# Four pass units of a decoder layer: float32 products replaced by split products, with the rests of their weights made on GpSimd

## The chip, the cores and the metric

The kernel runs on one core of a Trainium2 chip. Five engines each work through a queue of their own, in order: TensorE (PE, with its weight loads shown apart as PEld), VectorE (DVE), ScalarE (ACT), GpSimd (POOL) and SyncE (SP, which here only issues transfers). The metric is the device time of one execution in microseconds (us); lower is better. The median of three runs of the kernel before is 1585.19 us (1583.76 to 1586.9).

## The reference, cut to what matters

One decoder layer on 256 tokens of width 2048, all in float32: a conditioning vector gives six shift, scale and gate vectors, a normed and modulated input goes through one wide projection, and its parts feed a recurrent branch and an attention branch; then come an output projection and an MLP.

```python
mod = jnp.dot(c_act, w_ada[l]) + b_ada[l]
shift1, scale1, gate1, shift2, scale2, gate2 = jnp.split(mod, 6, axis=-1)
h = _modulate(_rms_norm(x, norm1_g[l]), shift1, scale1)
proj = jnp.einsum("bsd,de->bse", h, w_in[l])
lru_x, lru_gate, q, k, v, g_a, g_b = jnp.split(proj, split_idx, axis=-1)
...
```

The change is in the first part of `proj`: some products of `h` with columns of `w_in`.

## The kernel before

**Split products.** A float32 matrix product is put together from three products. Weights `w` and activations `h` are each split in a rounded part and a rest (`wh`, `wl` and `h[:, 0]`, `h[:, 1]`, of type float32r). `gemm` (lines 179 to 188) issues per tile of 128 rows `wh`·`h[:,0]` (L185), `wh`·`h[:,1]` (L186) and `wl`·`h[:,0]` (L187). The rounded half of a weight chunk of 128x1024 is made on ScalarE (`w_round`, L160), the rest `wl = raw - wh` on VectorE (`w_rest`, L165). `gemm_native` (L214) is the other way: it multiplies the raw weights with the unsplit activations `xs` in plain float32, with no preparation at all. In the trace each of its products shows as two records.

**The passes.** The conditioning matrix `w_ada` comes in 96 pieces of 1 MB, and each gives one column of `mod` on VectorE (`ada_unit`, L299). Tile j of `h` needs columns of two pieces: then `a` on VectorE (L314), the modulation and the rounding on ScalarE (L316, L318), the rest on VectorE (L322). While these tiles come into being one by one, TensorE already multiplies with those that exist. This is done in three passes over parts of the depth: tiles 0 and 1, tiles 2 to 5, tiles 6 to 9, for 56, 56 and 40 output tiles. A *pass unit* is one load of 1 MB of weights (2048 columns in `raw`, two chunks) for 16 products: pass one has units 0 to 6, pass two units 7 to 20 (four output tiles by four depth tiles each), pass three units 21 to 30. The table `NATIVE` names four units of pass two, with first output tile 0, 16, 32 and 48: units 7, 11, 15 and 19. They go through `gemm_native`. All others are split: `w_split` of the next unit is called one unit ahead. The sums of a unit leave PSUM (four buffers, `pg`) by VectorE in passes two and three (L399, L401).

**What sets the order.** Each engine's order is fixed when the program is built, by a scheduler that starts from the order of the code. Buffers come in rings: four for `raw` (weights and pieces of `w_ada` share them, names `rw` and `ra`), four each for `wh` and `wl`, so that two units are in the making or in use at a time. SyncE issues the loads; a load waits until the buffer's last user is done: for a split unit that is the rest's maker, for a native unit its last product.

**Behind the passes** comes `rel_lines` (lines 352 to 361): three small transfers issued from ScalarE's queue (L357), among them `onehot`, and a small product (L359) that needs them. Then the rest of the projection's depth follows from `w_r`, first for k and v.

Of the kernel before, what the change touches and what calls it, by code (L numbers as in the profile page):

```python
# [10 lines left out]
F32 = mybir.dt.float32  # L11
F32R = mybir.dt.float32r
AF = mybir.ActivationFunctionType
ALU = mybir.AluOpType
# [24 lines left out]
ZN_FROM = 9  # L39

PASSES = [(0, 2, 56), (2, 6, 56), (6, 10, 40)]
NATIVE = {(2, u) for u in range(0, 56, 16)}
NATIVE_REST = set()

ADA_ORDER = ([j + KT * s for j in range(KT) for s in (0, 1)] + [KT * s + j for s in (2, 4, 3, 5) for j in range(KT)])
# [13 lines left out]
def hybrid_layer(ctx: ExitStack, tc: tile.TileContext, x, xt, wada, w_p, w_r, w_f, vec, lruw, relb,  # L59
                 onehot, maskc, ident, out):  # L60
    nc = tc.nc
    te, ve, se = nc.tensor, nc.vector, nc.scalar
# [12 lines left out]
    def nm(s):  # L75
        cnt[0] += 1
        return f"{s}{cnt[0]}"

    def pair(dt=F32):
        return kp.tile([P, 2, T], dt, tag="k2", name=nm("k"))  # L80

    def tmp(shape=(P, 2, T), dt=F32):
        return tp.tile(list(shape), dt, tag="t2", name=nm("t"))
# [5 lines left out]
    pin = tc.keep_in_program_order  # L89
# [63 lines left out]
    def w_dma(src, n, pin=lambda i: i):  # L153
        raw = wp.tile([P, 2048], F32, tag="raw", name=nm("rw"), bufs=RAW_BUFS)
        pin(nc.sync.dma_start(out=raw[:, :n], in_=src))
        return raw, n

    def w_round(raw, o, c, pin=lambda i: i):
        wh = wp.tile([P, WCH], F32R, tag="wh", name=nm("wh"), bufs=WH_BUFS)
        pin(se.activation(wh[:, :c], raw[:, o:o + c], AF.Copy))  # L160
        return wh

    def w_rest(raw, o, c, wh, pin=lambda i: i):
        wl = wp.tile([P, WCH], F32R, tag="wl", name=nm("wl"), bufs=WH_BUFS)
        pin(ve.tensor_tensor(out=wl[:, :c], in0=raw[:, o:o + c], in1=wh[:, :c].bitcast(F32), op=ALU.subtract))  # L165
        return wh, wl

    def w_split(raw, n, pin=lambda i: i, o0=0):
        parts = []
        for o in range(o0, o0 + n, WCH):  # L170
            c = min(WCH, o0 + n - o)
            parts.append(w_rest(raw, o, c, w_round(raw, o, c, pin), pin))
        return parts

    def w_load(src, n):
        return w_split(*w_dma(src, n))

    def gemm(parts, o, acts):
        ps = pg.tile([P, T], F32, tag="pg", name=nm("pg"))
        n = len(acts)  # L180
        for k, hl in enumerate(acts):
            e = (o + k) * P
            wh, wl = parts[e // WCH]
            w = slice(e % WCH, e % WCH + P)
            te.matmul(ps, lhsT=wh[:, w], rhs=hl[:, 0], start=k == 0, stop=False)  # L185
            te.matmul(ps, lhsT=wh[:, w], rhs=hl[:, 1], start=False, stop=False)  # L186
            te.matmul(ps, lhsT=wl[:, w], rhs=hl[:, 0], start=False, stop=k == n - 1)  # L187
        return ps
# [20 lines left out]
    def gemm_native(raw, o, k0, k1):  # L209

        ps = pg.tile([P, T], F32, tag="pg", name=nm("pg"))
        for k in range(k0, k1):
            e = (o + k - k0) * P
            te.matmul(ps, lhsT=raw[:, e:e + P], rhs=xs[k // 2][:, k % 2], start=k == k0, stop=k == k1 - 1)  # L214
        return ps
# [50 lines left out]
    def turn_in(q, pin=lambda i: i):  # L266

        for j in (2 * q, 2 * q + 1):
            px = bank([P, 512])
            for i in range(2):  # L270
                for b in range(2):
                    e = (2 * (j % 2) + i) * P
                    te.transpose(px[:, i * T + b * P:i * T + (b + 1) * P], xtok[b, q][:, e:e + P], idt)
            xs.append(pair())
            pin(se.activation(xs[j].rearrange("p a b -> p (a b)"), px, AF.Copy))
# [27 lines left out]
    h = [None] * KT  # L303
    a1 = cp.tile([P, KT], F32, name="a1")

    def ada_norm1():
        n = ada_unit()
        if n % 2 == 1:
            norm1_tile(n // 2)
            norm1_rest(n // 2)  # L310
# [16 lines left out]
    raws = [w_dma(w_p[0], 2048, pin)]  # L327
# [7 lines left out]
    whs = w_round(raws[0][0], 0, WCH, pin)  # L335
    norm1_tile(0, pin)
    split_w = {0: [w_rest(raws[0][0], 0, WCH, whs, pin)]}
    norm1_rest(0, pin)
    ada_unit(pin)
    raws.append(w_dma(w_p[1], 2048, pin))  # L340
    split_w[0] += w_split(raws[0][0], WCH, pin, WCH)
    ada_unit(pin)
    norm1_tile(1, pin)
# [47 lines left out]
    def add_part(ps, f):  # L391
        sc_q = F_Q <= f < F_LX
        if f not in res:
            if f % 2 == 0:
                cur[0] = pair()
            res[f] = cur[0][:, f % 2]
            se.activation(res[f], ps, AF.Copy, scale=0.125 if sc_q else 1.0)
        elif sc_q:
            ve.scalar_tensor_tensor(out=res[f], in0=ps, scalar=0.125, in1=res[f], op0=ALU.mult, op1=ALU.add)  # L399
        else:  # L400
            ve.tensor_tensor(out=res[f], in0=ps, in1=res[f], op=ALU.add)  # L401


    p_units = [(k0, k1, u, min(KT // (k1 - k0), n - u))
               for k0, k1, n in PASSES for u in range(0, n, KT // (k1 - k0))]

    def pass_dma(i):
        k0, k1, u, nf = p_units[i]
        n = nf * (k1 - k0) * P
        raws.append(w_dma(w_p[i, :, 0:n], n))  # L410

    ada_due = 0.0
    for i, (k0, k1, u, nf) in enumerate(p_units):
        while len(raws) <= min(i + 1, len(p_units) - 1):
            pass_dma(len(raws))
        for j in (i, i + 1):
            if j < len(p_units) and j not in split_w and (p_units[j][0], p_units[j][2]) not in NATIVE:
                split_w[j] = w_split(*raws[j])
        while h[k1 - 1] is None:
            ada_norm1()  # L420
        for f in range(nf):
            kw = k1 - k0
            if (k0, u) in NATIVE:
                add_part(gemm_native(raws[i][0], f * kw, k0, k1), u + f)
            else:
                add_part(gemm(split_w[i], f * kw, h[k0:k1]), u + f)
        raws[i] = split_w[i] = None
        if i == 0:
            turn_in(2)
            turn_in(3)  # L430
        ada_due += ADA_FIRST
        while ada_due > 0 and ada_next[0] < 2 * KT:
            ada_norm1()
            ada_due -= 1
# [438 lines left out]
    for n in range(8):  # L873
        q, b = divmod(n, 2)
        pt = turned[n] if n < 2 else turn(n)
        o = tmp([P, 512])
# [97 lines left out]
```

## Time and profile before

| what | value |
|---|---|
| median of three runs | 1585.19 us |
| the profiled execution: its time, its span | 1588.35 us, 1586.0 us |
| granted TensorE clock, mean | 0.992 |
| HBM traffic over the span | 244 GB/s |
| the native units' first products at | 71.4, 97.05, 120.9 and 144.8 us |

Times in the views are microseconds from the span's start. In a timeline a row gives the start, the length, the engine, the line, the operation, what is written and read, how many were merged, and in brackets how long the engine had stood idle before it and what ended that. In a table of groups, the busy time and the mean of one in ns follow the count, then the idle time before. In a table of windows each engine has its busy time and, in brackets, its instructions; then come the granted clock, the share of the transfer engines and GB/s. A chain lists, in order of time, what the end was waiting for.

### The profile page before, as it was taken

Reading aid. Unit: us, or ns where it says so; the run is one execution under the profiler, and the core shown is the slowest. Engines: PE = TensorE matmul, PEld = TensorE weight load, DVE = VectorE, ACT = ScalarE, POOL = GpSimd, SP = SyncE. Lnnn points to the kernel's source line nnn. Section 1 sums busy time; section 2 is a strip of 40 time slices with the busy share of each in tenths; the row PEclk is TensorE's granted clock in tenths of the full one; section 3 lists DMA queues with packets and bytes.
Section 4 is the critical chain, followed back from the end, with each engine's and each line's share of the span. In section 5 each row is a group of like instructions: output and inputs, shape, how many; then the busy total and the mean of one; then the engine's idle time right before and its main releaser. Section 6 shows DMA issues by size and latency. Waiting matters only on the chain.

```text
span 1586.0 us, 24927 instructions
## 1 busy us (share of the span) xinstructions
PE 1545.5 (97%) x9812; PEld 1385.9 (87%) x9812; DVE 1217.2 (77%) x1941; ACT 886.2 (56%) x1510; POOL 0.2 (0%) x4
## 2 busy tenths in 40 slices
PE   5999999999999999999999999999999999999997
PEld 4999988899988888888889988888888888888886
DVE  6898988899999878789898877965565556655664
ACT  6733437686896564444456763356434663356553
POOL 0000000000000000000000000000000000000000
PEclk7999999999999999999999999999999999999999
DMA  8898976457867768777886666965555555555551
GB/s 343 332 350 333 341 257 224 173 181 244 302 244 282 281 239 313 277 292 285 329 301 239 235 246 244 348 233 186 186 186 188 188 189 187 189 191 191 190 187 54
DMA packets 61413, 387.89 MB, mean 245 GB/s; under 512 B 6800, under 2 KB 11248, under 8 KB 18928
## 3 DMA queue, kind: packets, MB, share of 16 engines
q1 hardware_dynamic: 56016, 380.83, 65.7%
q10 hardware_dynamic: 5280, 5.47, 1.1%
q8 instruction: 77, 1.26, 0.3%
q14 instruction: 40, 0.33, 0.1%
HBM read 384.13 MB, written 2.15 MB: 244 GB/s over the span
## 4 chain that ended last, share of the span: by engine, by line
PE 89%; DVE 5%; DMA 2%; ACT 2%; issue 1%; ACTq 0%; DVEq 0%
PE pg L199 45%; PE pg L198 21%; PE pg L187 5%; PE pg L185 5%; PE pg L186 5%; DVE ra L299 1%; PE pg L201 1%; DVE wl L165 1%; PE pg L214 1%; PE pg L762 1%; PE pg L763 1%; PE pg L764 1%; PE pa L575 1%; PE pa L568 1%; DMA ra<-in_wada_dram 1%
## 5 line engine op out<-in xcount | busy, mean ns | idle before, releaser
L199 PE MATMUL pg<-k,wh 128*128 128x512 f32 x3120 | 1078.9, 395 | 1.1 <-DVE k L149 1.1
L165 DVE TENSOR_TENSOR wl<-rw,wh 128x1024 fp32r<-128x1024 f32 (+2 forms) x534 | 625.9, 1178 | 270.9 <-ACT wh L160 261.3
L198 PE MATMUL pg<-k,wl 128*128 128x256 f32 x2925 | 819.2, 280 | 0.0
L160 ACT ACTIVATE wh<-rw 128x1024 fp32r<-128x1024 f32 (+2 forms) x534 | 542.3, 1021 | 491.3 <-PE pg L199 332.4
L199 PEld LDWEIGHTS pg<-k,wh 128*128 128x128 f32 x3120 | 572.7, 188 | 120.4 <-issue 1.4
L198 PEld LDWEIGHTS pg<-k,wl 128*128 128x128 f32 x2925 | 551.0, 188 | 9.7 <-ACT k L148 0.5
L185 PE MATMUL pg<-k,wh 128*128 128x256 f32 x832 | 238.3, 287 | 11.1 <-ACT k L318 9.7
L187 PE MATMUL pg<-k,wl 128*128 128x256 f32 x832 | 236.4, 284 | 2.1 <-DVE wl L165 2.1
L186 PE MATMUL pg<-k,wh 128*128 128x256 f32 x832 | 236.4, 284 | 0.0
L299 DVE CUSTOM_DVE_ANT_0 ra<-ra,scr,vc 128x2048 f32<-128x2048 f32 x96 | 224.8, 2344 | 4.3 <-DMA ra<-in_wada_dram 4.3
L185 PEld LDWEIGHTS pg<-k,wh 128*128 128x128 f32 x832 | 158.1, 190 | 14.1 <-ACT k L318 10.2
L187 PEld LDWEIGHTS pg<-k,wl 128*128 128x128 f32 x832 | 159.0, 191 | 3.8 <-DVE wl L165 2.7
L186 PEld LDWEIGHTS pg<-k,wh 128*128 128x128 f32 x832 | 158.4, 190 | 1.0 <-issue 0.7
L790 DVE SCALAR_TENSOR_TENSOR k<-pg,mod,k 128x256 f32<-128x256 f32 x128 | 61.9, 483 | 34.2 <-PE pg L199 32.0
L779 ACT ACTIVATE t<-t 128x256 f32<-128x256 f32 x55 | 23.0, 418 | 70.6 <-DVE t L206 70.5
L206 DVE TENSOR_TENSOR t<-pg,t 128x256 f32<-128x256 f32 x131 | 54.6, 417 | 0.3 <-ACT t L205 0.3
L201 PE MATMUL pg<-k,wl 128*128 128x256 f32 x195 | 54.5, 280 | 0.0
L205 ACT ACTIVATE t<-pg 128x256 f32<-128x256 f32 x131 | 47.7, 364 | 0.3 <-PE pg L199 0.3
L201 PEld LDWEIGHTS pg<-k,wl 128*128 128x128 f32 x195 | 36.6, 188 | 8.0
L763 PE MATMUL pg<-z,wh 128*128 128x256 f32 x144 | 40.9, 285 | 0.0
L762 PE MATMUL pg<-z,wh 128*128 128x258 f32 x144 | 40.9, 284 | 0.0
L764 PE MATMUL pg<-z,wl 128*128 128x258 f32 x144 | 40.7, 283 | 0.0
(163 smaller groups left out, 952.8 us busy)
## 6 DMA issues: line engine op xcount, KB each, us to landing
rw<-in_w_f_dram SPq DMA_DIRECT2D x204, 1024.0 KB, 4.9
ra<-in_wada_dram SPq DMA_DIRECT2D x96, 1024.0 KB, 6.3
rw<-in_w_p_dram SPq DMA_DIRECT2D x31, 1024.0 KB, 6.9
rw<-in_w_r_dram SPq DMA_DIRECT2D x20, 768.0 KB, 4.7
rw<-in_w_r_dram SPq DMA_DIRECT2D x16, 640.0 KB, 3.9
bt<-ud ACTq DMA_DIRECT2D x8, 512.0 KB, 3.9
lw<-in_lruw_dram SPq DMA_DIRECT2D x4, 512.0 KB, 5.3
k<-in_x_dram SPq DMA_DIRECT2D x8, 256.0 KB, 5.7
```

Of the source, the lines that this page charges most:

```text
L160: pin(se.activation(wh[:, :c], raw[:, o:o + c], AF.Copy))
L165: pin(ve.tensor_tensor(out=wl[:, :c], in0=raw[:, o:o + c], in1=wh[:, :c].bitcast(F32), op=ALU.subtract))
L185: te.matmul(ps, lhsT=wh[:, w], rhs=hl[:, 0], start=k == 0, stop=False)
L186: te.matmul(ps, lhsT=wh[:, w], rhs=hl[:, 1], start=False, stop=False)
L187: te.matmul(ps, lhsT=wl[:, w], rhs=hl[:, 0], start=False, stop=k == n - 1)
L198: te.matmul(ps[:, 0], lhsT=wl[:, w], rhs=hl[:, 0], start=False, stop=False)
L199: te.matmul(ps, lhsT=wh[:, w], rhs=hl, start=k == 0, stop=k == n - 1)
L201: te.matmul(ps[:, 0], lhsT=wl[:, w], rhs=hl[:, 0], start=False, stop=False)
L299: pin(ve.tensor_tensor_reduce(out=raw, in0=raw, in1=scr, scale=1.0, scalar=vc[:, V_BADA + c:V_BADA + c + 1], op0=ALU.mult, op1=ALU.add, ac ...
L762: te.matmul(ps, lhsT=wh[:, e], rhs=z[k][:, 0:258], start=k == 0, stop=False)
L763: te.matmul(ps[:, 0:256], lhsT=wh[:, e], rhs=z[k][:, 258:514], start=False, stop=False)
L790: ve.scalar_tensor_tensor(out=x1[f], in0=ps[:, i], scalar=mod[:, 5 * KT + f:5 * KT + f + 1], in1=x1[f], op0=ALU.mult, op1=ALU.add)
```

## The change

`NATIVE` becomes `POOL_REST`, and the four units are split like the others. Their rests are subtracted on GpSimd. No other unit's instructions change in kind or number. GpSimd gets eight subtractions of 128x1024, ScalarE eight roundings more, TensorE 192 split products in place of 64 plain ones. VectorE and SyncE have as many instructions as before.

```diff
-NATIVE = {(2, u) for u in range(0, 56, 16)}
+
+POOL_REST = {(2, u) for u in range(0, 56, 16)}
...
-    def w_rest(raw, o, c, wh, pin=lambda i: i):
+    def w_rest(raw, o, c, wh, pin=lambda i: i, eng=nc.vector):
         wl = wp.tile([P, WCH], F32R, tag="wl", name=nm("wl"), bufs=WH_BUFS)
-        pin(ve.tensor_tensor(out=wl[:, :c], in0=raw[:, o:o + c], in1=wh[:, :c].bitcast(F32), op=ALU.subtract))
+        pin(eng.tensor_tensor(out=wl[:, :c], in0=raw[:, o:o + c], in1=wh[:, :c].bitcast(F32), op=ALU.subtract))
         return wh, wl
-    def w_split(raw, n, pin=lambda i: i, o0=0):
+    def w_split(raw, n, pin=lambda i: i, o0=0, eng=nc.vector):
...
-            parts.append(w_rest(raw, o, c, w_round(raw, o, c, pin), pin))
+            parts.append(w_rest(raw, o, c, w_round(raw, o, c, pin), pin, eng))
...
-            if j < len(p_units) and j not in split_w and (p_units[j][0], p_units[j][2]) not in NATIVE:
-                split_w[j] = w_split(*raws[j])
+            if j < len(p_units) and j not in split_w:
+                split_w[j] = w_split(*raws[j], eng=nc.gpsimd if (p_units[j][0], p_units[j][2]) in POOL_REST else ve)
...
-            if (k0, u) in NATIVE:
-                add_part(gemm_native(raws[i][0], f * kw, k0, k1), u + f)
-            else:
-                add_part(gemm(split_w[i], f * kw, h[k0:k1]), u + f)
+            add_part(gemm(split_w[i], f * kw, h[k0:k1]), u + f)
```

The new file has one line more above these places, so that L165 becomes L166, L299 becomes L300 and so on; the texts below keep the numbers of the kernel before.

The scheduler also moves instructions of the other engines, from unit 7 to the middle of the projection's remaining depth. Two places matter below. The first is VectorE at unit 7. `wl_829` and `wl_833` are the rests of unit 8, the `ra` are pieces of `w_ada` (each with the reading of its sum, `ISA mod`), `a_153` and `k_843` belong to depth tile 5. Before:

```order
L165 TENSOR_TENSOR wl_829<-rw_825,wh_827 128x1024
L165 TENSOR_TENSOR wl_833<-rw_825,wh_831 128x1024
L299 ISA ra_835,mod<-ra_835,scr,vc 128x2048
L299 ISA ra_838,mod<-ra_838,scr,vc 128x2048
L314 SCALAR_TENSOR_TENSOR a_153<-mod,vc 128x1
L299 ISA ra_870,mod<-ra_870,scr,vc 128x2048
L322 TENSOR_TENSOR k_843<-k_215,k_843 128x256
```

The same place in the changed kernel, where the rests of unit 8 are called `wl_837` and `wl_841` and tile 5's is `k_851`:

```order
L166 TENSOR_TENSOR wl_837<-rw_833,wh_835 128x1024
L166 TENSOR_TENSOR wl_841<-rw_833,wh_839 128x1024
L300 ISA ra_843,mod<-ra_843,scr,vc 128x2048
L300 ISA ra_846,mod<-ra_846,scr,vc 128x2048
L300 ISA ra_910,mod<-ra_910,scr,vc 128x2048
L315 SCALAR_TENSOR_TENSOR a_153<-mod,vc 128x1
L323 TENSOR_TENSOR k_851<-k_215,k_851 128x256
```

A third piece of `w_ada` now stands ahead of `a`. The second place is ScalarE at the end of the passes, where `k_2309` is the rounding of the last depth tile. Before:

```order
L316 ACTIVATE k_330<-k_330,mod,a_153 128x256
L318 ACTIVATE k_2309<-k_330 128x256
L357 DMA relt<-in_relb_dram 32x32
L357 DMA t_2368<-in_onehot_dram 32x384
L357 DMA t_2369<-in_maskc_dram 32x384
L160 ACTIVATE wh_2421<-rw_2419 128x1024
```

In the changed kernel, where the same rounding writes `k_2469`:

```order
L317 ACTIVATE k_330<-k_330,mod,a_153 128x256
L161 ACTIVATE wh_2581<-rw_2579 128x1024
L319 ACTIVATE k_2469<-k_330 128x256
L358 DMA relt<-in_relb_dram 32x32
L358 DMA t_2528<-in_onehot_dram 32x384
L358 DMA t_2529<-in_maskc_dram 32x384
```

A rounding of weights of 128x1024 now stands ahead of the three transfers. On TensorE the product L359, which waits for `onehot`, moves too: before, two products of the remaining depth stood ahead of it, now fourteen do.

## The prediction

> **What bounds the kernel now.** I read the page's table of engines first, then windows over the passes, where the whole change lies, then the groups of VectorE there and the chain of waits behind them.
>
> ```profile
> PE 1545.5 (97%) x9812; PEld 1385.9 (87%) x9812; DVE 1217.2 (77%) x1941; ACT 886.2 (56%) x1510; POOL 0.2 (0%) x4
> 80.00:152.00 72.00, 72.00 (x531) 69.52 (x532) 64.77 (x100) 24.01 (x30) 0.00 (x0) 1.00 0.89 335
> 152.00:210.00 58.00, 58.00 (x494) 58.00 (x494) 56.90 (x86) 24.33 (x28) 0.00 (x0) 1.00 0.93 341
> ```
>
> Over the whole span TensorE is the bound and GpSimd does nothing. From 80 to 210 us (columns PE, PEld, DVE, ACT, POOL, clock, transfers) TensorE never stops; but VectorE is busy for 64.8 of 72 us and then for 56.9 of 58. There are two nearly full engines, and the saving comes on one of them only. What fills VectorE, 80 to 152 us:
>
> ```profile
> L165 DVE TENSOR_TENSOR wl<-rw,wh 128x1024 fp32r<-128x1024 f32 x20 | 23.7, 1216 | 1.1 <-ACT wh L160 1.1
> L299 DVE CUSTOM_DVE_ANT_0 ra<-ra,scr,vc 128x2048 f32<-128x2048 f32 x10 | 23.4, 2341 | 0.0
> L401 DVE TENSOR_TENSOR k<-pg,k 128x256 f32<-128x256 f32 x34 | 13.2, 416 | 3.6 <-PE pg L214 2.1 <-PE pg L187 1.4
> L399 DVE SCALAR_TENSOR_TENSOR k<-pg,k 128x256 f32<-128x256 f32 x16 | 6.3, 417 | 2.0 <-PE pg L187 1.9
> L322 DVE TENSOR_TENSOR k<-k,k 128x256 fp32r<-128x256 f32 x5 | 2.1, 418 | 0.5 <-ACT k L318 0.5
> ```
>
> Its idle time there is mostly waiting for sums of TensorE. Where both queues meet is at the end of the passes, in the chain:
>
> ```profile
> 209.76 0.15 DVE k L401
> 210.01 0.16 DVE a L314
> 210.19 0.61 ACT k L316
> 210.83 0.34 ACT k L318
> 211.21 6.20 DMA t<-in_onehot_dram
> 217.55 0.80 PE pa L359 x2
> ...
> 214.03 0.28 PE L186 MATMUL pg<-k,wh 128*128 128x256 f32 x1
> 217.55 0.80 PE L359 MATMUL pa<-t,relt 32*32 32x384 f32 x2 [3.24 <-DMA t<-in_onehot_dram]
> 219.00:223.00 4.00, 4.00 (x24) 4.00 (x23) 3.45 (x7) 2.13 (x4) 0.00 (x0) 0.58 0.70 219
> ```
>
> VectorE's `a` of the last depth tile, at 210.0, releases ScalarE, behind which the `onehot` transfer stands in the queue; TensorE's L359 starts 7.5 us behind `a`, after 3.24 us of standing still. Behind that pause the granted clock averages 0.58 for 4 us, so the pause costs some 4 x 0.42 = 1.7 us more. An earlier TensorE alone only waits longer here; `a` must come earlier too.
>
> **Part 1: TensorE's saving in units 11, 15 and 19.**
>
> ```profile
> 97.05 7.07 PE L214 MATMUL pg<-k,rw 128*128 128x256 f32 x32
> 103.77 0.47 PE L185 MATMUL pg<-k,wh 128*128 128x256 f32 x1
> 104.08 0.28 PE L186 MATMUL pg<-k,wh 128*128 128x256 f32 x1
> 79.98 0.39 PE L185 MATMUL pg<-k,wh 128*128 128x256 f32 x1 [0.37 <-DVE k L401]
> ```
>
> A native unit runs from 97.05 to one product (0.12) before 104.08: 6.9 us. A split unit is the rest: from 79.98 (unit 8) to 214.15 lie three native units, twenty split ones and two products behind them (0.24); (134.17 - 20.7 - 0.24) / 20 = 5.66 us. Saving 1.24 each, **3.7 us** for three.
>
> **Part 2: unit 7 gives its saving back.** The timelines of TensorE, VectorE and ScalarE there:
>
> ```profile
> 71.41 5.34 PE L214 MATMUL pg<-k,rw 128*128 128x256 f32 x24
> 77.62 1.99 PE L214 MATMUL pg<-k,rw 128*128 128x256 f32 x8 [0.87 <-ACT k L316]
> ...
> 70.97 1.23 DVE L165 TENSOR_TENSOR wl<-rw,wh 128x1024 fp32r<-128x1024 f32 x1 [0.27 <-ACT wh L160]
> 72.11 2.35 DVE L299 CUSTOM_DVE_ANT_0 ra<-ra,scr,vc 128x2048 f32<-128x2048 f32 x1
> 74.38 2.35 DVE L299 CUSTOM_DVE_ANT_0 ra<-ra,scr,vc 128x2048 f32<-128x2048 f32 x1
> 76.77 0.16 DVE L314 SCALAR_TENSOR_TENSOR a<-mod,vc 128x1 f32<-128x1 f32 x1
> 79.17 0.42 DVE L322 TENSOR_TENSOR k<-k,k 128x256 fp32r<-128x256 f32 x1
> 79.51 1.41 DVE L401 TENSOR_TENSOR k<-pg,k 128x256 f32<-128x256 f32 x4
> ...
> 69.86 1.07 ACT L160 ACTIVATE wh<-rw 128x1024 fp32r<-128x1024 f32 x1
> 76.96 0.60 ACT L316 ACTIVATE k<-k,mod,a 128x256 f32<-128x256 f32 x1 [4.98 <-DVE a L314]
> 77.60 0.42 ACT L318 ACTIVATE k<-k 128x256 fp32r<-128x256 f32 x1
> ```
>
> TensorE waits here for depth tile 5, that is for VectorE. Two things push it back. Unit 8's second rounding now finds its buffer in use until unit 6 ends at 71.4 (the ring of four holds units 6 and 7), so it runs 71.4 to 72.4 instead of from 69.86; its rest ends at 73.6 instead of 72.1: 1.5 us. And `a` now stands behind a third piece: three times 2.27 (the spacing from 72.11 to 74.38) from 73.65 gives `a` at 80.5 instead of 76.77. ScalarE needs from `a` to the rounding's end 1.25 us (76.77 to 78.02), then VectorE's rest: tile 5 is whole at 82.3, before at 79.6. The twelve products that need it were native before and could start on unsplit data at 77.62; now ten of them follow after 82.3, and unit 8 starts at about 83.6 instead of 79.98: **+3.6 us**. If a queue is later still (ScalarE's two extra roundings of 1.07 push four evictions each in pass one; the third piece's load now waits for GpSimd) it is 5; without the late rounding 2.
>
> **Part 3: ScalarE's eight roundings** cost 8 x 1.07 = 8.6 us on an engine that works 24 of 72 us; nothing waits, and TensorE covers them. The raw buffers of the four units come free earlier, at the rest instead of the last product, and loads start earlier: no cost; the transfers stand at 0.89 to 0.93.
>
> **Part 4: GpSimd beside VectorE.** The trace has no GpSimd operation on tiles. Its length is bounded by VectorE's rows: 1.22 us for the same subtraction, 2.34 for L299 on twice the elements; I take the long end, since this engine has shown nothing. TensorE would only wait for it above some 5 us each: the first rounding can start when its buffer comes free, one and a half units (8.5 us) ahead of the unit, and takes 1.07; the second rest is needed half a unit (2.8) into it; that leaves 8.5 - 1.07 + 2.8 = 10.2 us for two. What matters is VectorE beside it. Its operations L165, L299 and L322 read two tiles in SBUF, as the subtraction does: 23.7 + 23.4 + 2.1 of its 70.2 us, a share of 0.70; evictions read one. No row shows whether they disturb each other: the loss d per subtraction lies between 0 and 2.34 us (it can be no gain, since VectorE gives no work away). I choose that VectorE stands still wherever both want two tiles: 0.7 x 2.34 = 1.6 us. No row is near enough to decide this; it is a choice.
>
> [...]
>
> **The sum.** VectorE leaves unit 7 late by 3.4 us: the first sum is whole two products and their end behind tile 5, so its four evictions start at 82.9 instead of 79.5. Six subtractions beside units 9 to 19 add 6 x 1.6 = 9.6. What it can give back is its waiting for TensorE from 80 to 210 us, by the table of waits (total, times, longest):
>
> ```profile
> DVE k L401 <- PE pg L187: 2.2, 5, 0.9
> DVE k L401 <- PE pg L214: 2.1, 2, 1.2
> DVE k L399 <- PE pg L187: 1.9, 3, 1.0
> ```
>
> 6.2 us. So `a` of the last tile comes at 210.0 + 3.4 + 9.6 - 6.2 = 216.8, 6.8 late. The rounding put ahead of the transfers adds 1.07; twelve more products (1.4, at 5.66 / 48 each) now run ahead of L359 and are no longer behind it. That makes 6.8 + 1.07 - 1.4 = 6.5. As TensorE is delayed in the passes by the same VectorE, its pause before L359 may be shorter than 3.24 and the clock stay up: 0 to 1.7 back, I take 1.0. Result **+5.5 us**: 1588.35 + 5.5 = 1593.8 for the profiled execution. That one is 3.2 above the median of the runs; on the median it is 1593.8 - 3.2 = **1590.6**. Behind 223 us TensorE is again the engine that hardly stops, so a shift stays a shift; the moved order up to the middle of the remaining depth is worth one us or two either way.
>
> **Rivals.** *Undisturbed (d = 0):* VectorE then is no bound: `a` would be at 207.2 by it, but its last eviction ahead of `a` needs unit 29, which TensorE ends at 208.25 + 3.6 - 3.7 = 208.15; `a` at 208.7, 1.3 earlier. Then -1.3 + 1.07 - 1.4 = -1.6, and the pause falls to some 1.7 us, which may save the clock's 1.7: -1.6 to -3.3, in the middle **-2.5**, 1582.7. For it: 130 us in which GpSimd touches only eight tiles. The turning point is d = 0.7: below it the change does not lose. *The pause goes altogether:* if tile 5 is less late than worked out, L359 finds `onehot` there, and the 3.24 and 1.7 go: about -5, **1580**. Against it: the added rounding. *GpSimd is the bound:* above 5 us a subtraction TensorE waits in each of the four units; at 8 us 4 x (16 - 10.2) = 23 us, **1608**. No row speaks for such a length. *It takes no part of the path:* d near 0.7 in all, 1585.
>
> **How the numbers follow.** Forecast 0.45 (1587 to 1596, upper end d = 2.34: +4.4); undisturbed 0.28, split between faster and unchanged by the bound of 0.2% (3.2 us, about what a measurement of this kernel can tell from no change); pause gone 0.11; GpSimd the bound 0.04; nothing 0.12. The range leaves out GpSimd as bound and the ends of the two outer cases: 1580.2 to 1597. Faster: 0.11 + half of 0.28 = 0.25; slower: 0.45 + 0.04 - 0.03 of the forecast's low end = 0.46; same 0.29.
>
> **What would show it.** Unit 8's first product near 83.6 (part 2). Three times 1.24 us between unit starts (part 1). L165 and L299 longer than 1.2 and 2.34 us, or gaps before them, where a GpSimd row lies beside (part 4); if these stay as before, the undisturbed rival holds. `a` of the last tile at 216.8 or 208.7, and the idle time before L359. I am wrong if tile 5 is whole before 80, or if the stretch behind 223 us changes its length by more than 2 us.

## The result, and the profile after

The changed kernel takes 1601.14 us (median of four runs, 1594.93 to 1603.84), the kernel before 1584.85 (1583.76 to 1586.9): a ratio of 1.0093 with a 95% interval of 1.0074 to 1.0112. It is slower by some 15 us. The forecast of 1590.6 had the sign and a third of the size. The profiled execution of the changed kernel took 1601.39 us with a span of 1599.6, against 1588.35 and 1586.0 before.

The changed kernel's lines are numbered one higher (L165 is now L166, L299 is L300, L359 is L360). First its table of engines, and windows over the passes (columns: TensorE, weight loads, VectorE, ScalarE, GpSimd, clock, transfers):

```profile
PE 1546.3 (97%) x9876; PEld 1388.1 (87%) x9876; DVE 1224.9 (77%) x1941; ACT 895.4 (56%) x1518; POOL 25.7 (2%) x12
80.00:152.00 72.00, 67.86 (x552) 67.14 (x552) 67.64 (x94) 30.25 (x36) 20.72 (x6) 0.96 0.83 318
152.00:216.00 64.00, 63.34 (x535) 63.34 (x536) 63.55 (x99) 26.34 (x31) 0.00 (x0) 1.00 0.90 329
```

TensorE is busy for 0.8 us longer over the whole run (1546.3 us, before 1545.5), so 12.8 of the 13.6 us of span are standing still; what split products save is not to be seen in the busy time, as other products ran at a lower clock (0.96 on average in the first window). VectorE has the same 1941 instructions and is busier than before: 67.6 of 72 us, and behind it 63.6 of 64. The groups of the first window say why:

```profile
L300 DVE CUSTOM_DVE_ANT_0 ra<-ra,scr,vc 128x2048 f32<-128x2048 f32 x11 | 30.6, 2778 | 0.2 <-DMA ra<-in_wada_dram 0.2
L166 POOL TENSOR_TENSOR wl<-rw,wh 128x1024 fp32r<-128x1024 f32 x6 | 20.7, 3466 | 57.5 <-ACT wh L161 57.5
L166 DVE TENSOR_TENSOR wl<-rw,wh 128x1024 fp32r<-128x1024 f32 x16 | 20.4, 1290 | 0.0
```

A piece of `w_ada` takes 2.78 us on average where it took 2.34, a rest 1.29 where it took 1.22, and GpSimd needs 3.47 for one subtraction. Unit 7, on VectorE and then on TensorE, with a window behind it:

```profile
70.39 3.75 DVE L166 TENSOR_TENSOR wl<-rw,wh 128x1024 fp32r<-128x1024 f32 x2 [3.79 <-ACT wh L161]
...
80.89 0.15 DVE L315 SCALAR_TENSOR_TENSOR a<-mod,vc 128x1 f32<-128x1 f32 x1
82.15 0.43 DVE L323 TENSOR_TENSOR k<-k,k 128x256 fp32r<-128x256 f32 x1 [1.12 <-ACT k L319]
82.17 0.79 PE L186 MATMUL pg<-k,wh 128*128 128x256 f32 x2 [6.21 <-ACT k L319]
84.93 0.41 PE L186 MATMUL pg<-k,wh 128*128 128x256 f32 x1
82.00:86.00 4.00, 3.83 (x18) 3.83 (x18) 2.74 (x5) 2.17 (x3) 0.00 (x0) 0.50 1.01 422
```

`a` stands behind a third piece and comes at 80.9; TensorE waits 6.21 us for tile 5 and runs behind that at half its clock. The end of the passes, from the chain, the timeline and a window:

```profile
217.39 7.57 DMA t<-in_onehot_dram
225.10 0.80 PE L360 MATMUL pa<-t,relt 32*32 32x384 f32 x2 [4.17 <-DMA t<-in_onehot_dram]
225.00:229.00 4.00, 3.90 (x17) 3.31 (x18) 2.13 (x4) 0.37 (x1) 0.00 (x0) 0.63 0.40 110
```

L360 starts 7.55 us later than L359 did (217.55). That leaves the other half of the loss for the stretch behind it. The table of waits there, 225 to 440 us (total, times, longest):

```profile
PE pg L188 <- DVE wl L166: 7.3, 3, 2.9
DVE ra L300 <- DMA ra<-in_wada_dram: 14.7, 7, 4.2
```

The same two waits in the kernel before, over the same 225 to 440 us:

```profile
PE pg L187 <- DVE wl L165: 2.1, 3, 1.4
DVE ra L299 <- DMA ra<-in_wada_dram: 3.7, 3, 2.7
```

So the changed kernel loses in two places that lie apart, and the second lies behind the last changed unit.

### The profile page after: what moved, and what is told of

Same layout as the page of the kernel before. It is cut to its first block, busy times and chain, and to the rows that moved or that the text cites. A ratio compares the mean times of both kernels' runs of the same rounds, so it can differ in the third digit from the quotient of the medians.

```text
span 1599.6 us, 25100 instructions
## 1 busy us (share of the span) xinstructions
PE 1546.3 (97%) x9876; PEld 1388.1 (87%) x9876; DVE 1224.9 (77%) x1941; ACT 895.4 (56%) x1518; POOL 25.7 (2%) x12
## 3 DMA queue, kind: packets, MB, share of 16 engines
q8 instruction: 77, 1.26, 0.3%
## 4 chain that ended last, share of the span: by engine, by line
PE 84%; DVE 7%; DMA 4%; issue 2%; ACT 2%; POOL 0%; ACTq 0%; SPq 0%; DVEq 0%; POOLq 0%
PE pg L200 45%; PE pg L199 21%; PE pg L186 4%; PE pg L188 4%; PE pg L187 4%; DVE wl L166 2%; DVE ra L300 2%; DMA ra<-in_wada_dram 2%; PE pg L202 1%; PE pg L761 1%; PE pg L760 1%; PE pg L762 1%; ACT wh L161 1%; DVE t L534 1%; DMA rw<-in_w_p_dram 1%
## 5 line engine op out<-in xcount | busy, mean ns | idle before, releaser
L166 DVE TENSOR_TENSOR wl<-rw,wh 128x1024 fp32r<-128x1024 f32 (+2 forms) x534 | 628.9, 1183 | 268.4 <-ACT wh L161 261.9
L161 ACT ACTIVATE wh<-rw 128x1024 fp32r<-128x1024 f32 (+2 forms) x542 | 551.0, 1022 | 501.2 <-PE pg L200 327.8
L199 PE MATMUL pg<-k,wl 128*128 128x256 f32 x2925 | 818.4, 280 | 0.0
L200 PEld LDWEIGHTS pg<-k,wh 128*128 128x128 f32 x3120 | 572.3, 188 | 121.4 <-issue 1.4
L199 PEld LDWEIGHTS pg<-k,wl 128*128 128x128 f32 x2925 | 550.9, 188 | 9.5 <-ACT k L149 0.5
L186 PE MATMUL pg<-k,wh 128*128 128x256 f32 x896 | 258.3, 289 | 18.7 <-ACT k L319 15.0
L188 PE MATMUL pg<-k,wl 128*128 128x256 f32 x896 | 256.4, 287 | 7.3 <-DVE wl L166 7.3
L187 PE MATMUL pg<-k,wh 128*128 128x256 f32 x896 | 255.7, 286 | 0.0
L300 DVE CUSTOM_DVE_ANT_0 ra<-ra,scr,vc 128x2048 f32<-128x2048 f32 x96 | 229.7, 2395 | 17.9 <-DMA ra<-in_wada_dram 17.9
L186 PEld LDWEIGHTS pg<-k,wh 128*128 128x128 f32 x896 | 172.0, 192 | 21.5 <-ACT k L319 15.9
L188 PEld LDWEIGHTS pg<-k,wl 128*128 128x128 f32 x896 | 172.7, 193 | 10.2 <-DVE wl L166 7.9
L187 PEld LDWEIGHTS pg<-k,wh 128*128 128x128 f32 x896 | 172.7, 193 | 0.7 <-issue 0.5
L202 PE MATMUL pg<-k,wl 128*128 128x256 f32 x195 | 54.6, 280 | 0.0
L202 PEld LDWEIGHTS pg<-k,wl 128*128 128x128 f32 x195 | 36.6, 187 | 8.0
```

Of the source, the lines that this page charges most:

```text
L166: pin(eng.tensor_tensor(out=wl[:, :c], in0=raw[:, o:o + c], in1=wh[:, :c].bitcast(F32), op=ALU.subtract))
L199: te.matmul(ps[:, 0], lhsT=wl[:, w], rhs=hl[:, 0], start=False, stop=False)
L200: te.matmul(ps, lhsT=wh[:, w], rhs=hl, start=k == 0, stop=k == n - 1)
L202: te.matmul(ps[:, 0], lhsT=wl[:, w], rhs=hl[:, 0], start=False, stop=False)
L300: pin(ve.tensor_tensor_reduce(out=raw, in0=raw, in1=scr, scale=1.0, scalar=vc[:, V_BADA + c:V_BADA + c + 1], op0=ALU.mult, op1=ALU.add, ac ...
```

## The experiments

The theory was that some 6 us arise in the passes and some 8 in the remaining depth, the second from nothing but the moved order of the instructions there. Most kernels below put back, or keep, an order of VectorE, ScalarE and TensorE: the dependence of each instruction on its forerunner in the other kernel is written down for the scheduler, as a table behind the program:

```python
for a, b in zip(turn, turn[1:]):
    tc.add_manual_dep(mine[b], mine[a].name,
                      mybir.DependencyInfo(mybir.DependencyClass.NoSync, mybir.DependencyReason.DATA), reason="order")
```

The table of all runs follows; "passes" runs from `a` of depth tile 3 to `a` of the last tile, "behind" from there to the load with the number 99 among those named `rw` (counted from 0), both in the profiled execution, and "onehot" is its transfer there. For the second profile of the kernel before (e5) these rows are the ends:

```profile
53.29 0.16 DVE L314 SCALAR_TENSOR_TENSOR a<-mod,vc 128x1 f32<-128x1 f32 x1
209.91 0.15 DVE L314 SCALAR_TENSOR_TENSOR a<-mod,vc 128x1 f32<-128x1 f32 x1
577.73 0.33 SPq L155 DMA_DIRECT2D rw<-in_w_f_dram  x1
```

| kernel | median, us | ratio to before (interval) | passes | behind | onehot |
|---|---|---|---|---|---|
| before, first profile (execution of 1588.35) | 1584.85 | 1 | 156.3 | 371.7 | 6.20 |
| e5, before, second profile (1583.86) | | 1 | 156.6 | 367.8 | 4.15 |
| e6, before, third profile (1584.66) | | 1 | 156.3 | 367.7 | 4.00 |
| changed, first profile (1601.39) | 1601.14 | 1.0093 (1.0074 to 1.0112) | 162.1 | 380.4 | 7.57 |
| e9, changed again (1599.4) | 1598.47 | 1.0086 (1.0073 to 1.0100) | 161.8 | 378.5 | 5.34 |
| e1, order of before behind unit 19 | 1592.33 | 1.0045 (1.0030 to 1.0060) | 162.3 | 374.9 | 6.07 |
| e10, the same on VectorE alone | 1592.45 | 1.0047 (1.0034 to 1.0060) | 162.9 | 370.3 | 5.61 |
| e2, before in the order of the changed kernel | 1589.32 | 1.0033 (1.0020 to 1.0046) | 156.7 | 372.0 | 4.85 |
| e14, unit 7 alone | 1591.91 | 1.0048 (1.0036 to 1.0061) | 162.2 | 370.8 | 5.17 |
| e8, e1 with `a` of tile 5 first | 1592.09 | 1.0040 (1.0026 to 1.0054) | 162.4 | 370.6 | 4.49 |
| e4, e1 with unit 7 native | 1589.99 | 1.0033 (1.0021 to 1.0045) | 158.6 | 370.4 | 4.57 |
| e3, e1 with the rests on VectorE | 1590.10 | 1.0036 (1.0022 to 1.0049) | 160.0 | 370.8 | 4.42 |
| e13, both of these | 1588.91 | 1.0022 (1.0012 to 1.0032) | 155.4 | 373.1 | 6.08 |
| e7, before with GpSimd beside | 1590.74 | 1.0034 (1.0022 to 1.0046) | 161.5 | 368.9 | 4.15 |
| e12, before with writes of GpSimd beside | 1586.09 | 1.0009 (1.0000 to 1.0018) | 156.5 | 368.1 | 4.42 |
| e11, before with early loads | 1583.42 | 0.9991 (0.9982 to 1.0000) | 156.5 | 367.1 | 6.2 |
| e15, e13 with early loads | 1583.97 | 0.9991 (0.9983 to 1.0000) | 155.2 | 367.8 | 7.4 |

A ratio compares a kernel with executions of the kernel before from the same session; two medians of the table can come from different sessions, so that kernels are better compared by their ratios. How far single profiles of like passes differ is seen where units 7 to 19 are the same: 156.3 to 156.7 in the four profiles with those of before (e2 among them), 161.8 to 162.9 in the four with those of the changed kernel (e1 and e10 among them).

### The order behind the passes: e1, e2, e9, e10

e1 is the changed kernel with the table of before behind unit 19:

```diff
         (se if n % 2 else nc.sync).dma_start(out=out[b, :, q * 512:(q + 1) * 512], in_=o)
+    in_order(tc)
...
+TAIL = {
+    "DVE": (
+        "1-2 0 7 3-4 8 5 10 6 9 16 11-14 17 15 18-19 23 20-22 24 26-27 25 28-29 32 30-31 33-36 39 37-38 40 "
...
```

> The changed kernel, but everything behind unit 19 (units 20 to 30 of the passes and all that follows) stands on VectorE, ScalarE and TensorE in the order of the kernel before. Theory A (two parts: some +6 us arise in the passes, at unit 7 and where GpSimd runs beside VectorE; some +8 us more in the remaining depth, and those from the moved order alone): the first part stays, the second goes: +5 to +7 us against before, about 1591; the weight loads 51 to 99 come 5 to 7 us later than before, not 11 to 14. Theory B (knock-on: the late passes disturb the remaining depth by their lateness, loads meet other loads, whatever the order): +12 to +16, about 1599, loads 51 to 99 still 11 to 14 late.

It runs at 1592.33, by the ratios 7.1 us above before and 7.6 us below the changed kernel (8.8 by the medians, which come from two sessions). Its passes are as long as there (162.3), and of the waits for `wl` 1.9 us are left. Load 51 starts 7.0 us later than in the first profile of before (345.73 against 338.70); in the changed kernel it starts 11.3 later, and all three profiles have an onehot of over 6 us. By the time that is theory A, at the upper end of its 5 to 7. Load 99, though, is 9.2 us late (in the changed kernel 14.4), where A expected 5 to 7; this profile is that of e1's slowest execution (1596.47).

e2 is the kernel before with the other table in the same place.

> The kernel before (four native units, GpSimd idle), with everything behind unit 19 in the order of the changed kernel. Theory A: the order alone costs +6 to +9 us, about 1592, all of it between 230 and 410 us; waits for wl and for loads of ra as in the changed kernel. Theory B: 0 plus or minus 2 us, about 1585.

1589.32, 5.3 us above before (3.2 to 7.3): the order costs by itself, at the lower end of A's range or under it, and B, which expected nothing, falls. Whether the loss is smaller here than in the changed kernel, these intervals do not tell.

e9 is the changed kernel once more.

> The changed kernel once more, for a second profile. In its first one the onehot transfer took 7.57 us (4.0 to 4.5 in six other profiles, 6.1 to 6.2 in two), and behind 230 us TensorE stood still at four places (2.8, 1.6, 1.2, 2.9 us) where e1 stands still at none. Theory G (these four come from the order behind unit 19, not from a late onehot): they are there again; if onehot takes 4 to 4.5 us this time, the profiled execution is 1595 to 1598 and about 3.5 us below the first one. Rival H (the late onehot shifts the rest into a bad position): with an early onehot at least two of the four pauses are gone, and the time falls to e1's 1592.

Its onehot took 5.34 us, its profiled execution 1599.4, only 2.0 below the first; the four pauses are there again at 277, 304, 327 and 400 us (2.2, 2.0, 0.9, 1.2), with another of 0.8 at 237. G holds in kind; its 3.5 us was tied to an onehot of 4 to 4.5 us, which did not come. The table of waits for 230 to 420 us and the timelines at the first of the four show how the order makes a pause:

```profile
DVE ra L300 <- DMA ra<-in_wada_dram: 10.4, 6, 2.4
PE pg L188 <- DVE wl L166: 6.2, 5, 2.2
270.74 2.35 DVE L300 CUSTOM_DVE_ANT_0 ra<-ra,scr,vc 128x2048 f32<-128x2048 f32 x1 [0.64 <-DMA ra<-in_wada_dram]
...
273.13 0.30 DVE L534 CUSTOM_DVE_ANT_0 t<-pa,bt,vc 128x128 f32<-128x128 f32 x1
...
275.80 1.22 DVE L166 TENSOR_TENSOR wl<-rw,wh 128x1024 fp32r<-128x1024 f32 x1
277.07 0.39 PE L188 MATMUL pg<-k,wl 128*128 128x256 f32 x1 [2.18 <-DVE wl L166]
```

VectorE stands still until a piece of `w_ada` has arrived, works it off for 2.35 us, then eight rows of the attention's scores, and only then makes the rest for which TensorE has been waiting 2.18 us. In e1 VectorE waits once for such a load between 230 and 420 us (2.6 us); here six times, 10.4 us. A piece whose column is needed later holds up a rest that TensorE needs now.

e10 puts only VectorE's rows back.

> The changed kernel with VectorE alone put back into the order of before behind unit 19; the scheduler places the rest (which leaves 15 of ScalarE's 1303 rows and 70 of TensorE's 8704 in other places than before). Theory J (VectorE's order is what costs: pieces of w_ada and rests stand in another order, and a rest that TensorE needs comes late): as e1, 1590 to 1592, no pause over 1.5 us between 230 and 380 us. Rival K (the moved rows of TensorE and ScalarE cost as well): 1595 or more.

1592.45, as e1, with no pause over 1.32 us between 230 and 380: theory J. VectorE's order is enough to undo the loss. (Most of the moved rows of TensorE and ScalarE followed it back, so that a share of their own is not told apart.) e9 and e10 come from one session, and by their ratios the order costs 6.2 us.

About half of that is the clock. Behind the first two of e9's pauses (2.18 and 1.99 us) the granted clock averages 0.66 over 5 us, a loss of 1.7 us each; e10 has no such fall there. From `a` of the last tile to load 99, e9 stands still for 3.3 us longer and loses 5.1 us more to the clock, together 8.4, where the stretch is 8.2 us longer (378.5 and 370.3). But 1.7 of the 5.1 lie behind the pause at L360 (1.72 us in e9, 1.67 in e10, which left the clock at 1.00) and are not the order's. e2 has one such fall, behind a pause of 2.05 us at 270.

### The passes: e14, e8, e4, e3, e13

All of these have the order of before behind unit 19. e14 changes unit 7 alone:

```diff
+NATIVE = {(2, u) for u in (16, 32, 48)}
...
-            if j < len(p_units) and j not in split_w:
+            if j < len(p_units) and j not in split_w and (p_units[j][0], p_units[j][2]) not in NATIVE:
...
-            add_part(gemm(split_w[i], f * kw, h[k0:k1]), u + f)
+            add_part(gemm_native(raws[i][0], f * kw, k0, k1) if (k0, u) in NATIVE
+                     else gemm(split_w[i], f * kw, h[k0:k1]), u + f)
```

> Unit 7 alone split with its rests on GpSimd; units 11, 15 and 19 native; everything behind unit 19 in the order of before. Theory E (unit 7's delay is kept, since nothing behind it waits long): unit 8 starts 4 to 5 us late as in the changed kernel, `a` of the last tile still 3 to 5 us late, the time 4 to 6 us above before. Rival R (TensorE and VectorE make it up in units 8 to 30): `a` of the last tile less than 1.5 us late, the time within 2 us of before.

Theory E, and more of it than expected: the passes are 162.2 long, all that the changed kernel has, and the time is 1.0048 of before, 7.6 us. The window behind the pause:

```profile
83.00:87.00 4.00, 4.00 (x20) 4.00 (x21) 2.90 (x7) 2.11 (x2) 0.00 (x0) 0.50 1.01 426
```

Twenty products in four us, where there are 34 at the full clock (48 in 5.66 us).

e4 is the opposite, unit 7 native and the other three on GpSimd (`NATIVE = {(2, 0)}`).

> The changed kernel with unit 7 native again; units 11, 15 and 19 split with rests on GpSimd; everything behind unit 19 in the order of before. Theory E (unit 7 costs the passes +4 to +5 us by a tile 5 that comes late, and with the clock's fall behind that pause): about 5 us faster than e1, 1585 to 1587, about the time before; unit 8 starts near 80 us. Rival F (the disturbance of VectorE by GpSimd alone makes the end of the passes late, unit 7 is made up on the way): the same as e1 within 2 us, about 1590.

Passes of 158.6: 3.7 us less than e1, 2.0 more than before. The direction is E's. By the median it gains only 2.3 us (1.9 by the ratios) and stays 5.2 above before, where E expected about the time before; by the time alone rival F, within 2 us of e1, cannot be told from it. A second part remains, and the two do not add up: 2.0 and 5.6 alone, 5.7 together.

e8 takes 2 us of unit 7's pause away by putting `a` ahead of the third piece (some other rows of VectorE between units 7 and 19 changed places with it):

```diff
+        if n == 12:
+            tc.add_manual_dep(piece.ins, a_of[5].ins.name,
+                              mybir.DependencyInfo(mybir.DependencyClass.NoSync, mybir.DependencyReason.DATA), reason="a first")
```

> e1 (the changed kernel with the old order behind unit 19), with `a` of tile 5 put ahead of the third piece on VectorE at unit 7. Theory E (the pause at unit 7 is carried to the end of the passes): tile 5 whole 2.3 us earlier, unit 8 starts 2.3 us earlier than in e1, `a` of the last tile 2 us earlier, the time 2 to 3 us below e1. Rival F (VectorE's whole length of work sets the end of the passes, wherever it pauses): unit 8 earlier, but `a` of the last tile and the time within 1 us of e1.

`a` of tile 5 comes at 79.15 instead of 81.01, and the passes stay at 162.4, the time at 1592.09. This is rival F. TensorE's pause falls from 6.18 to 4.03 us, but of the gain 1.1 us are left at the start of unit 8 (83.93 against 85.05) and none at `a` of tile 6 (91.63 against 90.86), before GpSimd's next subtraction starts at 95.09: the piece that was passed over stands ahead of tile 6 all the same. Later VectorE's rows beside the last six subtractions are stretched by 10.0 us in all, in e1 by 8.5. VectorE's length of work is then the likely second limit, just behind the first; which share GpSimd has in it, this run does not tell.

e3 has all four units split, their rests on VectorE (`POOL_REST = set()`).

> The changed kernel with the eight rests of the four units on VectorE (GpSimd idle), everything behind unit 19 in the order of before. Theory C (GpSimd's subtractions take from VectorE 1.2 to 1.3 us each by contention, as much as the 1.22 us that each takes on VectorE itself): within 2 us of e1 in either direction, about 1591. Theory D (GpSimd spares VectorE most of it, or costs TensorE elsewhere): over 4 us slower than e1, or over 3 us faster.

1590.10, 2.2 us below e1, where theory C had 2 as its bound and D over 3; by the time that decides for neither. The passes are 2.3 shorter than with GpSimd.

e13 takes both out: units 11, 15 and 19 split with rests on VectorE, unit 7 native.

> Units 11, 15 and 19 split with their rests on VectorE (six rests, 7.3 us more work for it), unit 7 native, GpSimd idle, everything behind unit 19 in the order of before. Theory P (unit 7 costs some 4 us of the passes and GpSimd's blocking some 2; VectorE's own rests fit into its waiting for TensorE): `a` of the last tile within 1.5 us of the usual execution of before (209.9), the time 1583 to 1587. Rival Q (VectorE is full, each rest comes out in full whoever is spared): `a` 4 us or more late, the time 1589 or more.

`a` of the last tile comes at 210.09 and the passes shrink to 155.4, 1.2 us under e5. For the passes that is theory P; the time, 1588.91, lies 1.9 us above P's range and just short of Q's 1589. Against e4 it is the price of GpSimd for the same six rests, by itself: the passes are 158.6 - 155.4 = 3.2 us longer with GpSimd than with the rests on VectorE, which spends 7.3 us on them (by the ratios the times differ by 1.7). Of TensorE's expected 3.7 us, 1.2 arrive at `a`. Why the time is nonetheless above before is answered by the last group.

### GpSimd beside VectorE: e7, e12

e7 leaves the kernel before as it is, order included, and adds two subtractions on GpSimd per native unit, whose result nobody reads:

```diff
+                for o in (0, WCH):
+                    nc.gpsimd.tensor_tensor(out=aside, in0=raws[j][0][:, o:o + WCH], in1=raws[j][0][:, o:o + WCH], op=ALU.subtract)
```

> The kernel before, its units 7, 11, 15 and 19 native, every row of VectorE, ScalarE, TensorE and SP in its order; GpSimd alone is added: two subtractions on each of the four native units' weights (1024 elements, two inputs in SBUF, output to a tile that nobody reads yet). It is the price of GpSimd's presence alone. Theory C (each subtraction costs VectorE 1.2 to 1.5 us): the rows of VectorE beside it grow by 8 to 12 us in all, `a` of the last tile comes 2 to 5 us later, the time is 2 to 5 us above before. Rival (contention takes only VectorE's spare time): `a` within 1 us, the time within 1 us of before.

The passes are 4.9 us longer, the time 1.0034 of before (5.4 us): theory C, at or just over its upper end. VectorE's rows beside the subtractions are 8.9 us longer in all, 1.1 for each, within its 8 to 12. Eight subtractions that serve nothing cost that much. In e12 GpSimd only reads one column and then writes four times 128x1024:

```diff
+                nc.gpsimd.tensor_copy(aside[:, 0:1], raws[j][0][:, 0:1])
+                for _ in range(4):
+                    nc.gpsimd.memset(aside, 0.0)
```

> e7 with another load on GpSimd: for each of the four native units one copy of 128x1 elements (which waits for the weights) and four memsets of 128x1024, that read nothing, in place of the two subtractions. All other rows in the order of before. Theory N (VectorE is blocked because both engines read SBUF through something that they share): the memsets cost nothing, VectorE's rows beside them keep their lengths, the time is that of before plus or minus 1 us. Rival O (any work of GpSimd beside VectorE costs): rows grow as in e7, 2 to 6 us above before.

The passes are 156.5, as before; the time is 1.0009 of before (1.4 us, interval 1.0000 to 1.0018): N, or just over its 1 us. Timelines at unit 10, first of e7, then of e12:

```profile
93.89 4.86 POOL L425 TENSOR_TENSOR aside<-rw 128x1024 f32<-128x1024 f32 x2 [25.20 <-DMA rw<-in_w_p_dram]
96.90 4.00 DVE L299 CUSTOM_DVE_ANT_0 ra<-ra,scr,vc 128x2048 f32<-128x2048 f32 x1
```

```profile
91.07 2.34 DVE L299 CUSTOM_DVE_ANT_0 ra<-ra,scr,vc 128x2048 f32<-128x2048 f32 x1
91.56 1.89 POOL L424 COPY aside<-rw 128x1 f32<-128x1 f32 x1 [22.64 <-DMA rw<-in_w_p_dram]
93.52 3.99 POOL L426 MEMSET aside<- 128x1024 f32 x4
96.32 2.34 DVE L299 CUSTOM_DVE_ANT_0 ra<-ra,scr,vc 128x2048 f32<-128x2048 f32 x1
```

In e7 GpSimd works until 98.75, and the piece that VectorE takes up at 96.90 ends at 100.90: 98.75 + 2.34 is 101.1, so it stood nearly still until GpSimd was done. In e12 the copy of a single column lasts 1.89 us, until the piece that ran when it started ends at 93.41; beside the four writes a piece takes its 2.34. In these rows operations that read on both sides exclude each other as wholes (the piece takes 4.00 us in e7), and writes exclude nothing (2.34 in e12); what the two engines share is not shown. An eviction reads one tile in SBUF: of 84 that lie beside a subtraction of GpSimd, in seven runs, none took over 0.43 us. All stretched rows read two (L165, L299, L314 and L322 in the numbers of before).

### The kernel before a second and third time, and the early loads: e5, e6, e11, e15

> The kernel before, once more, for a second profile: its profiled execution (1588.35) was the slowest of its runs but for none, and e2, e3 and e4 read nearly the same in their profiles (1588.5 to 1589.7) though they are 5 to 6 us slower by the medians. Theory: a usual execution of the kernel before lies near 1584 because the pause ahead of L359 is shorter (1 to 2 us instead of 3.24) and the clock stays up behind it; TensorE's wait for onehot then reads 1 to 2 us. Rival: the 3 to 4 us lie elsewhere, and that wait reads 3.2 again.

> The kernel before a third time, for a third profile, to the same question as the run ahead of it: wait for onehot 1 to 2 us where the time is near 1584, 3.2 us where it is near 1588.

They took 1583.86 and 1584.66, and TensorE's wait for onehot was 1.2 and 1.0 us. From e5, the chain, TensorE's timeline and a window:

```profile
211.11 4.15 DMA t<-in_onehot_dram
215.40 0.80 PE L359 MATMUL pa<-t,relt 32*32 32x384 f32 x2 [1.20 <-DMA t<-in_onehot_dram]
219.00:223.00 4.00, 4.00 (x36) 4.00 (x36) 3.91 (x12) 1.61 (x2) 0.00 (x0) 1.00 0.95 346
```

The transfer is issued 1.20 us behind `a` as in the first profile (211.11 and 211.21), but lasts 4.15 us and not 6.20, and the clock stays at 1.00 where it averaged 0.58. The pause of 3.24 us from which the forecast argued belonged to the profiled execution and is not the usual one. Behind `a` lie 3.9 of the 4.5 us between the two executions (371.7 and 367.8), 2.0 of them in the longer pause and some 1.7 in the clock. Other pauses at L359 or L360, rows of e3 and of e8, each with its window:

```profile
219.70 0.80 PE L360 MATMUL pa<-t,relt 32*32 32x384 f32 x2 [1.42 <-DMA t<-in_onehot_dram]
220.00:224.00 4.00, 4.00 (x32) 3.57 (x31) 3.46 (x6) 2.49 (x4) 0.00 (x0) 1.00 0.50 141
```

```profile
222.27 0.80 PE L364 MATMUL pa<-t,relt 32*32 32x384 f32 x2 [1.49 <-DMA t<-in_onehot_dram]
222.00:226.00 4.00, 3.73 (x18) 3.14 (x19) 2.89 (x4) 1.72 (x3) 0.00 (x0) 0.70 0.51 145
```

A pause of 1.42 us left the clock alone, one of 1.49 brought it down to 0.70 on average. The usual pause of before, 1.0 to 1.2, is a little shorter than the shortest behind which the clock fell in any of the profiles, 1.36 (last section).

e11 loads the three tiles in unit 22, and everything else stays in its place:

```diff
+        if i == 22:
+            rel_loads()
```

> The kernel before with relt, onehot and maskc loaded in unit 22 (some 50 us earlier) instead of at the end of the passes; every row of the engines in its order. It looks for a version that beats both. Theory L (the pause ahead of L359 is the transfer's, 1.0 to 1.2 us in usual executions and 3.2 with the clock's fall in others): 1 to 1.5 us below before, near 1583, and no execution over 1585.5. Rival M (another wait takes its place, `a` of the last tile or VectorE's product of the sum): 0 plus or minus 0.7 us.

1583.42, 1.5 us below the medians of before of that session (1584.9), a ratio of 0.9991 (0.9982 to 1.0000); of 11 executions none is over 1584.93, where before reached 1588.51. Theory L: the wait is gone, and with it the long executions, though onehot's transfer itself took 6.2 us here.

> e13 with relt, onehot and maskc loaded in unit 22, as in e11. If theory P holds: 1 to 1.5 us below e13 by the pause ahead of L359, and no execution with the late transfer; 1582 to 1585. If TensorE's saving of 3.7 us comes through in full, 1580 to 1582, and the kernel beats both. Rival Q: 1588 or more.

1583.97: 4.9 us below e13, and no execution over 1585.0. So what e13 lost hung on the late loads. In its profile, that of its slowest execution, the pause at L361 is 3.21 us, with the clock's fall; TensorE stops 4.2 us behind `a` there, in the kernel before 4.3, so it is a transfer of 6.08 us that makes the pause long, and no gain of TensorE's over `a`. Why none of e13's eight executions is below 1586.32 is not shown. Yet e15 is no faster than e11, at the same ratio to before; of the 1.3 us by which its passes are shorter, 0.7 are lost again by load 99 (367.8 and 367.1 behind). So what splitting brings, with the costs that were found taken out, is nothing that these runs can tell from zero. e11 and e15 lie under both kernels, by 0.0009 under the one before, with an interval that ends at 1.

## Why the prediction was wrong, and where it was right

**The step that failed** is the last sentence of the sum: "Behind 223 us TensorE is again the engine that hardly stops, so a shift stays a shift; the moved order up to the middle of the remaining depth is worth one us or two either way." The order was seen to move, and was given a price without a row. It cost 6.2 us by the ratios of e9 and e10, 7.6 by those of the changed kernel and e1, and 5.3 in the kernel before; by the profiles 6.7 (e9 and e10, without the clock behind L360) and 5.5 (380.4 and 374.9 behind `a`, the changed kernel's first profile and e1's). TensorE hardly stopped there because VectorE made its rests in time (2.1 us of waiting for them from 225 to 440 us); that is a property of the old order. In the moved order it waits for rests that stand behind pieces of `w_ada` (7.3 us), and two of the pauses brought its clock down (0.66 over the 5 us behind each). The prediction's own test said that it is wrong if that stretch changes by more than 2 us, and it changed by 8.7 (371.7 and 380.4).

**Part 1 held.** Counted by their products, units 11 and 12 take 12.56 us in e5 (6.72 and 5.84) and 11.30 in e15 (5.65 each): 1.26 saved, forecast 1.24. But units 16 to 21 of e15 take 5.87 to 6.35 us, where TensorE waits for VectorE's sums, and so little of it arrives.

**The sum of the passes held as a number, in part by luck.** `a` of the last tile was to come at 216.8 and came at 215.71; L360 was to be 6.5 us late, counting 1.4 for the twelve products ahead of it, and was 7.55 - 1.4 = 6.15. But the rounding put ahead of the transfers moved their issue by 0.5 us, not by 1.07 (1.68 behind `a`, before 1.20), and 1.4 of the 7.55 come from a transfer that lasted 7.57 us instead of 6.20, which nothing in the sum foresaw. e1, in which only the passes are changed, lies 7.1 us above before by its ratio (4.8 to 9.5); the forecast was 5.5.

**Part 2 was right in mechanism, too small in size.** Tile 5 was whole at 82.6 (82.15 and 0.43), forecast 82.3, `a` at 80.89, forecast 80.5; but unit 8 started at 84.93, not 83.6, as the products behind the pause run at half the clock (window 82 to 86: 0.50; over the passes the clock loses 3.4 us). That fall is not in part 2, though the prediction had used the same fall at L359. Nor was it seen that this delay alone makes a loss as large as all parts together: e14's passes are 5.6 us longer, those of the changed kernel 5.2 and 5.5.

**Part 3 stood:** TensorE waits for a rounding for 0.6 us in the whole of the changed run.

**Part 4 was right in kind.** d was chosen as 1.6 us, with no row that showed it. In the changed kernel the six rows of VectorE beside the last six subtractions are longer than their usual lengths by 7.9 us in all (from 0.4 to 2.2), 1.3 per subtraction; a subtraction alone takes 2.4 (2.39 to 2.41), where d was worked out from 2.34, and up to 4.45 when it is the one that waits. What was wrong is the adding: 3.4 for unit 7 and 9.6 for GpSimd less 6.2 of waiting came near the measured sum with shares that do not add, and that is luck. By e4 and e14 they overlap (2.0 and 5.6 give 5.7); that VectorE is then blocked in time that the late unit 8 has lost already is the likely reason, but only argued.

**The clock's 1.0 back** came from an unusual execution. In usual ones the pause is 1.0 to 1.2 us and there was no fall to win back. It was the other way: the changed kernel's pauses (1.72 and 4.17 us) brought the clock down.

**Rivals.** Undisturbed VectorE is ruled out by e7, GpSimd as the bound by its rows (at most 4.45 us in the changed kernel, where the prediction had 5 as the limit). No rival had the moved order as its mechanism, and the range ended at 1597 because nothing but a GpSimd of over 5 us per operation was seen to lead beyond it.

**Open** is how unit 7's and GpSimd's shares of the passes overlap, why e13 loses at the late loads in every execution, and what makes onehot's transfer last 4.0 us at one time and 6.2 or 7.6 at another; none of this was tried.

## What to carry to other kernels

When a change makes a scheduler move instructions far behind the place that was edited, put the old order back there before judging the edit: here a little under half of the loss came from the order alone. Moving subtractions of two inputs from VectorE to GpSimd did not relieve VectorE here, which in the kernel before reads two tiles itself for 0.70 of its work (L165, L299 and L322, 49.2 of 70.2 us from 80 to 152 us): with six of them on GpSimd the passes were 3.2 us longer than with the same six on VectorE itself (158.6 and 155.4). And profile the kernel before more than once before arguing from a pause in it.

## What was not expected of the hardware

The clock fell behind quite short pauses of TensorE, the shortest of 1.36 us (e7: 0.74 on average from 221 to 225 us). Windows behind the pauses at L360 of e9 (1.72 us) and at L361 of e14, and the latter's row:

```profile
220.00:230.00 10.00, 8.28 (x54) 7.32 (x53) 6.25 (x11) 3.30 (x5) 0.00 (x0) 0.83 0.81 283
```

```profile
222.78 0.80 PE L361 MATMUL pa<-t,relt 32*32 32x384 f32 x2 [2.22 <-DMA t<-in_onehot_dram]
223.00:227.00 4.00, 4.00 (x19) 3.49 (x18) 3.38 (x4) 1.72 (x3) 0.00 (x0) 0.59 0.34 69
```

All pauses of TensorE over 0.9 us behind the first 70 us, in the seventeen profiles, with the clock granted in the 5 us behind each, give this: of those up to 1.32 us, 44 in number, none brings the clock down; of 17 from 1.36 to 1.72 us 4 do (1.36, 1.49, 1.69 and 1.72, while 1.42, 1.67 and 1.70 do not); of 18 from 1.99 to 6.21 us all but one (2.58). All four of the 17 stand at the product with onehot, where 4 of 7 pauses of this length bring the clock down; none of the 10 before other rows does. What sets these apart is not shown. So a wait that grew by 0.5 us, from the usual 1.2 to e9's 1.72, cost some 1.7 us more (0.17 of 10 us). And beside GpSimd the smallest operations were held up too; a row of VectorE in the changed kernel:

```profile
102.29 1.67 DVE L315 SCALAR_TENSOR_TENSOR a<-mod,vc 128x1 f32<-128x1 f32 x1
```

`a`, 0.15 us long elsewhere, stood still for 1.5 us beside a subtraction.
